# Two layers of a hybrid trunk on one core: attention scores in float32r on 64 rows, GLA in 64-row blocks, token-major columns in groups of 512

## The chip, the cores and the metric

The kernel runs on one core of one Trainium2 chip. The metric is the device time of one execution in microseconds (us); of several executions the median counts. TensorE multiplies matrices, VectorE and ScalarE do the elementwise work, GpSimd very little of it, and SyncE issues the transfers of the weights. In the rows of the trace these are PE (its weight loads PEld), DVE, ACT, POOL and SP.

## What is computed

Two layers over 256 tokens with 1024 channels. Each layer is an FFN, a mixer, a second FFN and a small per-layer embedding, each with a residual and a layer norm. The change lies in the mixer alone:

```python
(a_x, a_y, b_q, b_k, b_v, b_low, b_r,
 c_q, c_k, c_v, c_f, gate_logits) = split(x @ w_in)
y_a = gelu(a_y) * rg_lru(conv(a_x), ...)               # 512 channels
y_b = gla(b_q, b_k, b_v, b_low, w_g2, b_g, norm_g, b_r)
y_c = forgetting_attention(c_q, c_k, c_v, c_f, b_f)
merged = sum(sigmoid(gate_logits)[n] * (y_n @ w_branch[n]) for n in 0, 1, 2)
out = merged @ w_out
# gla: 4 heads, keys of 64, values of 128, chunks of 64 tokens
g = log_sigmoid(b_low @ w_g2 + b_g) / 16; G = cumsum(g within a chunk)
state = scan(exp(G_end), (b_k * exp(G_end - G)).T @ b_v)     # one per chunk
o = (b_q / 8) @ state; y_b = o * rsqrt(mean(o*o) + eps) * norm_g * silu(b_r)
# forgetting attention: 8 heads of 64, queries in two blocks of 128 tokens
F = cumsum(log_sigmoid(c_f + b_f))
s = c_q @ c_k.T / 8 + F[query] - F[key]; y_c = softmax(causal(s)) @ c_v
```

## The kernel before

**Products.** Every large product is made of three products in float32r. A weight piece `raw` arrives by a transfer (16 buffers in turn), ScalarE rounds it to `whi` (line 194), VectorE computes the rest `wlo` (line 195), and TensorE adds hi x hi, hi x lo and lo x hi in PSUM. `mm_tok` (lines 296 to 298) puts tokens on the partitions and weight columns in the free dimension ("token-major"); `mm_feat` (lines 308 to 310) puts 128 weight columns on the partitions and the 256 tokens in the free dimension. The activations are `XH` and `XL`. Products that need more precision with few columns (states, scores, values of attention) are plain float32, which TensorE runs in two passes; a float32 MATMUL of the program therefore counts as x2 in a row of the trace.

**Order.** The instruction order of each engine is the order in which the program is written. The mixer runs a list of units. A unit is one group of weight products (some 48, about 5.7 us each). `run(unit, *new)` adds new chains, lets every live chain do one step, and then emits the unit. A chain is a generator whose `yield` ends a step, so that what a chain needs next from another engine has the time of one unit to be made.

**The mixer's units.** Token-major columns come in `b` groups of 436, 436 and 432 (keys and values of GLA, low-rank decay input, output gate of GLA, forget logits; the array `tm` holds them), and the values of attention in two units `v` of 256. Between these stand two `ax` units (convolution input), two `ay` units (the gate of the first branch), the queries `bq` of GLA, and queries `cq` and keys `ck` of attention, two units each. The chains: `gla_decays` (through `w_g2`, the log-sigmoid at lines 558 to 560 and the exponential at 591 and 593 to the decayed keys), `fox_forget` (the sums F, cast to bfloat16 in three pieces at line 623, transposed at 629), `gla_gate` (line 740), `lru` (lines 671 to 687), `gla_states` (line 718, then the updates over chunks), `gla_out` (line 754, squares, then the products with the norm and the gate at line 260, and the transposes `to_feat` at line 378) and `fox_attend` (scores at lines 786 to 790, softmax, values at 818). After these units come the merge units: 12 gate units and 4 branch units, among whose steps attention is spread.

**GLA products.** The keys are masked to a chunk's half of 128 tokens and the queries `bq` are padded with zeros to 128 rows, so that each product uses 128 rows and 64 columns of the array.

**Scores.** For a head, one bfloat16 product adds -F of the keys, one or two add F of the queries, one adds the causal mask, and one float32 product adds queries times keys; the queries `qz` are padded with zeros to 128 rows, two heads' keys lying above each other. One PSUM bank of 512 columns holds four heads' scores at the first 128 tokens, two at the second: six calls of `fox_attend` per layer, one at every second merge unit.

## Time and profile before

| | |
|---|---|
| median of 3 runs | 1331.17 us (1330.39 to 1331.78) |
| profiled execution, and its span | 1329.03 us, 1327.3 us |
| PE busy | 1306.4 us (98%) |
| PEld busy | 1231.0 us (93%) |
| DVE busy | 825.4 us (62%) |
| ACT busy | 663.9 us (50%) |
| POOL busy | 48.2 us (4%) |
| mean granted clock of TensorE | 0.996 |

The span is what the profile covers of its execution. Busy shares are means over stretches of different kinds. A MATMUL's duration in a row is from its start to its modelled end, and the next begins before that; the price of one among many is the distance of the starts. PEclk is the granted clock as a share of the upper of TensorE's two levels, 2.4 GHz.

### The profile page before, as it was taken

How to read it: one execution, taken by the hardware profiler on the slowest of the kernel's cores; microseconds unless marked ns; L12 is line 12 of the kernel's file. 1: busy time of each engine (PE TensorE's matmuls, PEld its weight loads, DVE VectorE, ACT ScalarE, POOL GpSimd, SP SyncE). 2: the span in 40 equal slices, each digit the busy share in tenths (PEclk: the TensorE clock that was granted, in tenths of full speed). 3: DMA queues.
4: the chain of work that ended last, by engine and by line, in shares of the span. 5: the costliest groups of instructions: out<-in, count | busy, mean ns of one | idle time of the engine just before them, and what ended most of it. 6: DMA issues, size and time to landing. Idle time of an engine off the chain costs nothing. (4 is left out here: it accounts for less than half of the span.)

```text
span 1327.3 us, 22841 instructions
## 1 busy us (share of the span) xinstructions
PE 1306.4 (98%) x9492; PEld 1231.0 (93%) x9492; DVE 825.4 (62%) x1015; ACT 663.9 (50%) x869; POOL 48.2 (4%) x46
## 2 busy tenths in 40 slices
PE   8999999999999999999899999999999999999996
PEld 8999999999999999998799999899999989999985
DVE  6665567675657755557774556676755586555576
ACT  6554436965445444444354445279654444444541
POOL 0000000000001000000000000100000010000000
PEclk9999999999999999999999999999999999999998
DMA  8855736445466466674565667464554555566732
GB/s 273 293 194 190 246 120 236 160 160 162 156 187 199 139 200 184 190 235 168 175 206 182 188 189 244 145 195 154 182 159 147 193 189 168 183 188 188 252 129 72
DMA packets 70216, 246.18 MB, mean 185 GB/s; under 512 B 8160, under 2 KB 8672, under 8 KB 70112
## 3 DMA queue, kind: packets, MB, share of 16 engines
q1 hardware_dynamic: 69824, 244.33, 57.1%
q8 instruction: 74, 1.21, 0.4%
q10 hardware_dynamic: 288, 0.39, 0.1%
q14 instruction: 30, 0.25, 0.1%
HBM read 243.64 MB, written 1.05 MB: 184 GB/s over the span
## 5 line engine op out<-in xcount | busy, mean ns | idle before, releaser
L195 DVE TENSOR_TENSOR wlo<-raw,whi 128x1024 fp32r<-128x1024 f32 (+3 forms) x442 | 541.5, 1234 | 401.1 <-ACT whi L194 399.5
L194 ACT ACTIVATE whi<-raw 128x1024 fp32r<-128x1024 f32 (+3 forms) x442 | 459.6, 1047 | 447.4 <-PE ps L309 263.2
L308 PE MATMUL ps<-XH,whi 128*128 128x256 f32 x1888 | 534.5, 283 | 5.4 <-ACT whi L194 5.4
L310 PE MATMUL ps<-XH,wlo 128*128 128x256 f32 x1888 | 530.5, 281 | 0.4 <-DVE wlo L195 0.4
L309 PE MATMUL ps<-XL,whi 128*128 128x256 f32 x1888 | 530.4, 281 | 0.0
L308 PEld LDWEIGHTS ps<-XH,whi 128*128 128x128 f32 x1888 | 356.6, 189 | 7.8 <-ACT whi L194 5.4
L309 PEld LDWEIGHTS ps<-XL,whi 128*128 128x128 f32 x1888 | 356.4, 189 | 1.4
L310 PEld LDWEIGHTS ps<-XH,wlo 128*128 128x128 f32 x1888 | 356.6, 189 | 0.8 <-DVE wlo L195 0.8
L296 PE MATMUL ps<-whi,XH 128*128 128x256 f32 (+3 forms) x488 | 162.4, 333 | 0.0
L298 PE MATMUL ps<-whi,XL 128*128 128x256 f32 (+3 forms) x488 | 159.0, 326 | 1.3 <-DVE XL L260 1.2
L297 PE MATMUL ps<-wlo,XH 128*128 128x256 f32 (+3 forms) x488 | 159.1, 326 | 0.0
L296 PE MATMUL ps<-whi,hh 128*128 128x512 f32 x368 | 144.6, 393 | 0.0
L298 PE MATMUL ps<-whi,hl 128*128 128x512 f32 x368 | 143.7, 391 | 0.0
L297 PE MATMUL ps<-wlo,hh 128*128 128x512 f32 x368 | 143.3, 389 | 0.0
L298 PEld LDWEIGHTS ps<-whi,XL 128*128 128x128 f32 x488 | 92.0, 189 | 8.2 <-DVE XL L260 1.7
L297 PEld LDWEIGHTS ps<-wlo,XH 128*128 128x128 f32 x488 | 92.4, 189 | 6.2 <-DVE wlo L195 0.3
L296 PEld LDWEIGHTS ps<-whi,XH 128*128 128x128 f32 x488 | 92.0, 188 | 6.6 <-ACT tm L553 0.3
L298 PEld LDWEIGHTS ps<-whi,hl 128*128 128x128 f32 x368 | 69.1, 188 | 15.2 <-DVE hl L260 0.2
L297 PEld LDWEIGHTS ps<-wlo,hh 128*128 128x128 f32 x368 | 69.3, 188 | 13.1
L296 PEld LDWEIGHTS ps<-whi,hh 128*128 128x128 f32 x368 | 69.1, 188 | 12.8
L269 ACT ACTIVATE hh<-w 128x512 fp32r<-128x512 f32 x40 | 25.1, 632 | 71.7 <-DVE w L260 71.7
L308 PE MATMUL ps<-yh,whi 128*128 128x256 f32 x192 | 54.9, 286 | 0.0
(160 smaller groups left out, 953.5 us busy)
## 6 DMA issues: line engine op xcount, KB each, us to landing
raw<-in_wu SPq DMA_DIRECT2D x414, 512.0 KB, 4.1
gb<-in_lnp SPq DMA_DIRECT2D x16, 512.0 KB, 5.9
raw<-in_wu SPq DMA_DIRECT2D x16, 436.0 KB, 4.4
raw<-in_wu SPq DMA_DIRECT2D x8, 432.0 KB, 4.1
xr<-in_xT SPq DMA_DIRECT2D x4, 256.0 KB, 4.4
raw<-in_wu SPq DMA_DIRECT2D x4, 256.0 KB, 4.7
XR<-in_x SPq DMA_DIRECT2D x1, 1024.0 KB, 7.3
wa<-in_lru SPq DMA_DIRECT2D x2, 512.0 KB, 3.8
```

The costliest lines, as they stand in the source:

```text
L194: self.nc.scalar.activation(hi[:, c], raw[:, c], AF.Copy)
L195: (lo or self.nc.vector).tensor_tensor(out=lw[:, c], in0=raw[:, c], in1=hi[:, c].bitcast(F32), op=ALU.subtract)
L269: S.activation(hi, src, AF.Copy)
L296: TE.matmul(o, lhsT=lh[:, k, c], rhs=hi[:, kk, :], start=start and kk == 0, stop=False)
L297: TE.matmul(o, lhsT=lh[:, k, c], rhs=lo[:, kk, :], start=False, stop=False)
L298: TE.matmul(o, lhsT=ll[:, k, c], rhs=hi[:, kk, :], start=False, stop=stop and kk == kt - 1)
L308: TE.matmul(o, lhsT=hi[:, kk, c], rhs=rh[:, k, :], start=start and kk == 0, stop=False)
L309: TE.matmul(o, lhsT=hi[:, kk, c], rhs=rl[:, k, :], start=False, stop=False)
L310: TE.matmul(o, lhsT=lo[:, kk, c], rhs=rh[:, k, :], start=False, stop=stop and kk == kt - 1)
```

## The change

Token-major columns are cut into groups of 512, 512, 280 and 512. The first two are GLA's values (in an array `gv` of their own) and its output gate; the third holds the low-rank input, the forget logits and GLA's keys; the fourth the values of attention. The third moves ahead of the convolution units, the fourth stands where the `v` units stood. Some chains start at another unit.

GLA's products use 64 rows and 64 columns: a chunk's keys and values lie on 64 rows, two chunks in the two row halves and two heads in the two column halves. The keys need one product instead of two masked ones, the queries no padding.

In the scores, one bfloat16 product with per-head factors (`fQ`, made by eight operations of 256 columns on VectorE, and `fK`) adds both forget terms, one adds the mask. Queries and keys of attention are split into two float32r parts, and three products of 64 rows per head replace the float32 one; two heads run in the two row halves of the array, each into a PSUM bank of its own. `fox_attend` handles two banks at a time, so it is called three times per layer, at every fourth merge unit.

```diff
-FOX_EVERY = 2
+FOX_EVERY = 4
...
+
+PB = (0, 512, 1024, 1304, 1816)
+TM_LOW, TM_CF, TM_K, TM_R, TM_CV, TM_N = 0, 16, 24, 280, 792, 1304
+TM_AT = (None, TM_R, TM_LOW, TM_CV)
...
+        b_group(2)
         for i in range(2):
...
         for i in range(2):
             w_in(l, "ay", i, C_AY)
-        for i in range(2):
-            out.append(((l, "v", i), "w_in", (l,), 0, D, C_CV + 256 * i, 256, "k"))
+        b_group(3)
...
-                S.activation(tm[:, t, PB[g]:PB[g + 1]], acc[g, t][:, :n], AF.Copy)
+                S.activation(tm[:, t, TM_AT[g]:TM_AT[g] + n] if g else gv[:, t, :], acc[g, t][:, :n], AF.Copy)
...
-            gla["kd"] = []
-            for h in range(2):
-                k = work()
-                stt(k.rearrange("p (t c) -> p t c", t=2), e.rearrange("p (t c) -> p t c", t=2), chunk[:, h:h + 1],
-                    tm[:, :, TM_K:TM_K + 256], ALU.mult, ALU.mult)
-                gla["kd"].append(k)
+            gla["kd"] = work()
+            tt(gla["kd"].rearrange("p (t c) -> p t c", t=2), e.rearrange("p (t c) -> p t c", t=2), tm[:, :, TM_K:TM_K + 256], ALU.mult)
...
                 V.tensor_copy(part, fc3)
+                V.tensor_copy(fcat[:, :, 32 + 8 * i:40 + 8 * i], fc3)
...
-            fox["f"] = mt([P, T], BF16, "fT")
-            fox["nf"] = mt([P, T], BF16, "nfT")
-            V.tensor_copy(fox["f"], o16[:, :T])
-            ts(fox["nf"], o16[:, :T], -1.0, None, ALU.mult)
+            f = mt([P, T], BF16, "fT")
+            V.tensor_copy(f, o16[:, :T])
+            fox["k"] = mt([P, T], BF16, "fK")
+            ts(fox["k"], f, fox_kmul, fox_kadd, ALU.mult, ALU.add)
+            fox["q"] = mt([P, NH, T], BF16, "fQ")
+            for h in range(NH):
+                if h == NH // 2:
+                    yield
+                ts(fox["q"][:, h, :], f, fox_mul[:, h:h + 1], fox_add[:, h:h + 1], ALU.mult, ALU.add)
...
-        def unit_q(key, dst, h0):
-            o = feat(key)
-            for h in range(4):
-                r = slice((h % 2) * 64, (h % 2) * 64 + 64)
-                S.activation(dst[r, h0 + h, :], o[r, (h // 2) * T:(h // 2 + 1) * T], AF.Copy, scale=0.125)
+        def unit_bq():
+            S.activation(flat(bq), feat((l, "bq", 0)), AF.Copy, scale=0.125)
+
+        def unit_cq(i):
+            o = feat((l, "cq", i))
+            hi, lo = (flat(x[:, 2 * i:2 * i + 2, :]) for x in q2)
+            S.activation(hi, o, AF.Copy, scale=0.125)
+            stt(lo, o, 0.125, hi.bitcast(F32), ALU.mult, ALU.subtract)
...
-            for n in range(4):
-                t, h = n // 2, n % 2
+            for t in range(2):
                 for hd in range(4):
-                    pr, r = hd // 2, slice((hd % 2) * 64, (hd % 2) * 64 + 64)
-                    at = (pr * 2 + t) * P
-                    TE.matmul(od[h][r, at:at + P], lhsT=kd[h][:, t * 256 + hd * 64:t * 256 + hd * 64 + 64],
-                              rhs=tm[:, t, TM_V + hd * P:TM_V + (hd + 1) * P], start=True, stop=True)
+                    for h in range(2):
+                        pr, r, k = hd // 2, rows[hd % 2], rows[h]
+                        at = (pr * 2 + t) * P
+                        TE.matmul(od[h][r, at:at + P], lhsT=kd[k, t * 256 + hd * 64:t * 256 + hd * 64 + 64],
+                                  rhs=gv[k, t, hd * P:(hd + 1) * P], start=True, stop=True)
...
             for t in range(2):
-                o = ps()
-                for hd in range(4):
+                for r in range(2):
...
-                        TE.matmul(o[h * 64:(h + 1) * 64, hd * P:(hd + 1) * P], lhsT=bq[:, hd, n * 64:(n + 1) * 64],
-                                  rhs=gla["st"][n][:, hd // 2, :], start=True, stop=True)
-                os.append(o)
-            for t in range(2):
+                        for e in range(2):
+                            TE.matmul(os[e][rows[h], (2 * t + r) * P:(2 * t + r + 1) * P], lhsT=bq[rows[e], r, n * 64:(n + 1) * 64],
+                                      rhs=gla["st"][n][rows[e], r, :], start=True, stop=True)
...
-            o = ps()
+            os = [ps() for _ in range(2)]
+            at = [slice(j * kn, (j + 1) * kn) for j in range(nh)]
             for j in range(nh):
-                h = g * nh + j
-                c = o[:, j * kn:(j + 1) * kn]
-                TE.matmul(c, lhsT=sel16[:, h, :], rhs=fox["nf"][:, :kn], start=True, stop=False)
-                for i in range(t + 1):
-                    TE.matmul(c[:, i * P:(i + 1) * P], lhsT=fox["f"][:, tk], rhs=sel16[:, h, :], start=False, stop=False)
-                TE.matmul(c[:, tk], lhsT=ident16, rhs=mask16, start=False, stop=False)
-                TE.matmul(c, lhsT=qz[:, h, tk], rhs=kT[:, :t + 1, h // 2, :], start=False, stop=True)
-            mx = small(4, tag="mx")
-            V.tensor_reduce(out=mx[:, :nh], in_=o.rearrange("p (h c) -> p h c", h=nh), axis=mybir.AxisListType.X, op=ALU.max, negate=True)
-            yield
-            pr = work()
-            sums = small(4, tag="sums")
+                for e in range(2):
+                    c = os[e][:, at[j]]
+                    TE.matmul(c, lhsT=fox["q"][:, 2 * (g * nh + j) + e, tk], rhs=fox["k"][:, :kn], start=j == 0, stop=False)
+                    TE.matmul(c[:, tk], lhsT=ident16, rhs=mask16, start=False, stop=False)
...
+                for n, (x, y) in enumerate(((0, 0), (0, 1), (1, 0))):
+                    for e in range(2):
+                        TE.matmul(os[e][:, at[j]], lhsT=q2[x][rows[e], g * nh + j, tk], rhs=fox["kk"][y][rows[e], (g * nh + j) // 2, (g * nh + j) % 2, :kn],
+                                  start=False, stop=n == 2 and j == nh - 1)
...
+        run(lambda: [b_both(2, h) for h in range(2)])
         run(lambda: unit_ax(0))
         run(lambda: unit_ax(1), gla_decays())
-        run(b2)
-        run(lambda: unit_ay(0), lru(0), fox_forget(), gla_gate())
-        run(lambda: unit_ay(1))
-        run(lambda: unit_v(0))
-        run(lambda: unit_v(1), lru(1), gla_states())
-        run(lambda: unit_q((l, "bq", 0), bq, 0))
-        run(lambda: unit_q((l, "cq", 0), qz, 0))
+        run(lambda: unit_ay(0), fox_forget(), gla_gate())
+        run(lambda: unit_ay(1), lru(0))
+        run(lambda: b_both(3, 0))
+        run(lambda: b_both(3, 1), lru(1))
+        run(unit_bq, gla_states())
+        run(lambda: unit_cq(0))
         run(lambda: unit_k(0), gla_out())
...
-        attend = [(0, 0), (0, 1), (1, 0), (1, 1), (1, 2), (1, 3)]
...
-            run(f, *([fox_attend(*attend.pop(0))] if attend and n % FOX_EVERY == 0 else []))
+            run(f, *([fox_attend(*attend.pop(0))] if attend and n % FOX_EVERY == 2 else []))
```

**ScalarE, layer 0, around the exponential of the decays.** The queue before, from two weight splits to the forget logits' second table load. In the names, `whi` and `raw` are weights, `w` work buffers, `s` small ones; ACT_TABLE_LOAD loads the table of the function that follows it.

```order
L194 ACTIVATE whi_2545<-raw_2544 128x1024
L194 ACTIVATE whi_2575<-raw_2574 128x1024
L658 ACT_TABLE_LOAD
L658 ACTIVATE w_2580<-ps_2519 128x512
L591 ACT_TABLE_LOAD
L591 ACTIVATE w_2590<-ps_2582 128x512
L593 ACTIVATE s_2592<-ps_2585 128x8
L558 ACTIVATE w_2597<-s_2513 128x16
L559 ACTIVATE w_2598<-w_2597 128x16
L560 ACT_TABLE_LOAD
L560 ACTIVATE w_2598<-w_2598 128x16
```

The same queue now, from the gelu of the first `ay` unit (line 655) to the second `lru` function's table; the exponential of the decays (line 591 before, 586 now) follows seven rows further.

```order
L655 ACT_TABLE_LOAD
L655 ACTIVATE w_2559<-ps_2498 128x512
L553 ACTIVATE w_2562<-s_2492 128x16
L554 ACT_TABLE_LOAD
L554 ACTIVATE w_2563<-w_2562 128x16
L555 ACT_TABLE_LOAD
L555 ACTIVATE w_2563<-w_2563 128x16
L668 ACT_TABLE_LOAD
L668 ACTIVATE w_2571<-ps_2574,vec 128x256 x2
L668 ACTIVATE w_2572<-ps_2577,vec 128x256 x2
L671 ACTIVATE w_2573<-w_2571,lruc 128x256 x2
L673 ACT_TABLE_LOAD
```

The forget logits' log-sigmoid (lines 553 to 555) and the first `lru` chain (668 to 673) now stand ahead of the decays' exponential; before, the former stood behind it and the latter further ahead.

**VectorE, layer 0, ahead of the GLA output's transposes.** Before, the last twelve rows up to the products with the gate; `wlo` are weight remainders, `yl` the end of an `lru` chain.

```order
L195 TENSOR_TENSOR wlo_3061<-raw_3059,whi_3060 128x1024
L195 TENSOR_TENSOR wlo_3091<-raw_3089,whi_3090 128x1024
L763 TENSOR_REDUCE s_3098<-w_3030 128x4
L763 TENSOR_REDUCE s_3098<-w_3032 128x4
L266 TENSOR_SCALAR s_3098<-s_3098 128x8
L195 TENSOR_TENSOR wlo_3130<-raw_3128,whi_3129 128x1024
L195 TENSOR_TENSOR wlo_3160<-raw_3158,whi_3159 128x1024
L260 TENSOR_TENSOR yl_2256<-w_2402,yh_2255 128x512
L260 TENSOR_TENSOR w_3030<-ps_3012,s_3098 128x512
L260 TENSOR_TENSOR w_3032<-ps_3021,s_3098 128x512
L260 TENSOR_TENSOR w_3030<-w_3030,tm_2072 128x512
L260 TENSOR_TENSOR w_3032<-w_3032,tm_2072 128x512
```

Now, from the first splits behind the state updates on, `fT`, `fK` and `fQ` being the forget factors and `ql` the remainder of attention's queries; the products with the norm and the gate stand some ten rows further.

```order
L198 TENSOR_TENSOR wlo_2841<-raw_2839,whi_2840 128x1024
L198 TENSOR_TENSOR wlo_2871<-raw_2869,whi_2870 128x1024
L623 COPY fT_2879<-ps_150_2876 128x256
L269 TENSOR_SCALAR fK_2881<-fT_2879,cf 128x256
L269 TENSOR_SCALAR fQ_2883<-fT_2879,cf 128x256 x4
L198 TENSOR_TENSOR wlo_2917<-raw_2915,whi_2916 128x1024
L198 TENSOR_TENSOR wlo_2947<-raw_2945,whi_2946 128x1024
L266 SCALAR_TENSOR_TENSOR ql_2073<-ps_2890,qh_2072 128x512
L269 TENSOR_SCALAR fQ_2883<-fT_2879,cf 128x256 x4
L263 TENSOR_TENSOR yl_2253<-w_2396,yh_2252 128x512
L263 TENSOR_TENSOR w_2709<-w_2709,w_2710 128x512
L684 SCALAR_TENSOR_TENSOR w_2475<-w_2708,w_2709 128x256 x2
```

Eight factor products and the queries' remainder stand ahead of the last rows of an `lru` chain, where before only a copy and a negation of the transposed sums stood.

**TensorE, layer 0, scores at the second 128 tokens.** Before, one head's rows; `nfT` and `fT` are the forget sums, `cb` the identity, mask and selection matrices.

```order
L786 LDWEIGHTS cb_85
L786 MATMUL ps_3639<-nfT_2939,cb_85 128x256
L788 LDWEIGHTS fT_2938
L788 MATMUL ps_3639<-cb_85,fT_2938 128x128
L788 LDWEIGHTS fT_2938
L788 MATMUL ps_3639<-cb_85,fT_2938 128x128
L789 LDWEIGHTS cb_85
L789 MATMUL ps_3639<-cb_85 128x128
L790 MATMUL ps_3639<-tm_2072,qz_2074 128x256
```

Now, the end of the bfloat16 rows of the first four heads and their float32r products; `wa` and `gv` hold the two parts of attention's keys, `qh` and `ql` those of its queries.

```order
L796 LDWEIGHTS fQ_2883
L796 MATMUL ps_3606<-fK_2881,fQ_2883 128x256
L797 LDWEIGHTS cb_85
L797 MATMUL ps_3606<-cb_85 128x128
L801 MATMUL ps_3605<-wa_2984,qh_2072 128x256
L801 MATMUL ps_3606<-wa_2984,qh_2072 128x256
L801 MATMUL ps_3605<-gv_2985,qh_2072 128x256
L801 MATMUL ps_3606<-gv_2985,qh_2072 128x256
L801 MATMUL ps_3605<-wa_2984,ql_2073 128x256
L801 MATMUL ps_3606<-wa_2984,ql_2073 128x256
```

The float32r products of two heads alternate, each head's into a bank of its own.

## Rows read from the trace of the kernel before

**Rows 1.** Waits of PE: engine, line, waited for; us in total, times, longest.
```profile
PE ps L378 <- DVE XR L263: 2.1, 1, 2.1
```

**Rows 2.** Windows in layer 0's mixer; columns stand in the first line.
```profile
core 0: us, PE busy (x) PEld busy (x) DVE busy (x) ACT busy (x) POOL busy (x), PEclk, DMA share, GB/s
237.00:267.00 30.00, 30.00 (x257) 29.16 (x256) 18.62 (x30) 29.71 (x46) 2.79 (x2) 1.00 0.50 171
317.00:417.00 100.00, 100.00 (x863) 97.25 (x862) 58.81 (x71) 46.63 (x75) 8.70 (x6) 1.00 0.54 169
```

**Rows 3.** Timeline of PE: start us, us, engine, line, operation, out<-in, count.
```profile
203.31 0.45 PE L296 MATMUL ps<-whi,XH 128*128 128x436 f32 x1
...
214.08 0.28 PE L308 MATMUL ps<-XH,whi 128*128 128x256 f32 x1
...
219.78 0.38 PE L571 MATMUL ps<-cf,tm 128*128 128x128 f32 x2
...
652.63 0.39 PE L298 MATMUL ps<-whi,XL 128*128 128x512 f32 x1
...
654.03 0.40 PE L298 MATMUL ps<-whi,XL 128*128 128x512 f32 x1
```

**Rows 4.** Timeline of DVE and PE at three hand-offs of layer 0's mixer.
```profile
254.55 1.21 DVE L195 TENSOR_TENSOR wlo<-raw,whi 128x1024 fp32r<-128x1024 f32 x1
255.69 1.40 DVE L263 SCALAR_TENSOR_TENSOR w<-w,cf,tm 128x512 f32<-128x512 f32 x2
...
258.32 1.97 PE L718 MATMUL ps<-tm,w 128*64 128x128 f32 x32
...
270.59 0.17 DVE L623 CAST fcat<-s 128x16 bf16<-128x16 f32 x1
...
272.38 0.28 PE L629 MATMUL ps<-cb,fcat 128*128 128x128 bf16 x2
...
295.85 1.28 DVE L260 TENSOR_TENSOR w<-w,tm 128x512 f32<-128x512 f32 x2
...
297.38 0.60 PE L378 MATMUL ps<-cf,w 128*128 128x128 f32 x4
```

**Rows 5.** Timeline of ACT; in brackets the idle time ahead and its releaser.
```profile
226.67 0.58 ACT L647 ACTIVATE axp<-ps 128x512 f32<-128x512 f32 x1
...
232.59 4.59 ACT L194 ACTIVATE whi<-raw 128x1024 fp32r<-128x1024 f32 x4 [0.54 <-PE ps L298]
...
249.65 0.60 ACT L591 ACTIVATE w<-ps 128x512 f32<-128x512 f32 x1
...
252.10 1.99 ACT L194 ACTIVATE whi<-raw 128x1024 fp32r<-128x1024 f32 x2
...
254.12 1.28 ACT L658 ACT_TABLE_LOAD   x1
```

**Rows 6.** Groups by line, DVE, shapes apart: busy us, mean ns | idle us before.
```profile
L266 DVE TENSOR_SCALAR w<-w,s 128x256 f32<-128x256 f32 x16 | 4.9, 351 | 0.3
```

**Rows 7.** Timeline of PE in attention: scores of four heads, values, scores of two.
```profile
303.89 0.22 PE L786 MATMUL ps<-nfT,cb 128*128 128x128 bf16 x1
...
304.06 0.44 PE L790 MATMUL ps<-tm,qz 128*128 128x128 f32 x2
...
305.58 0.36 PE L308 MATMUL ps<-XH,whi 128*128 128x256 f32 x1
...
330.36 0.28 PE L310 MATMUL ps<-XH,wlo 128*128 128x256 f32 x1
330.56 0.66 PE L818 MATMUL ps<-w,tm 128*64 128x128 f32 x8
331.15 0.28 PE L786 MATMUL ps<-nfT,cb 128*128 128x256 bf16 x1
...
332.50 0.47 PE L308 MATMUL ps<-yh,whi 128*128 128x256 f32 x1
```

**Rows 8.** Windows at the border of the two layers, columns as in rows 2.
```profile
654.00:657.30 3.30, 1.20 (x8) 0.73 (x7) 3.27 (x8) 0.00 (x0) 0.92 (x1) 1.00 0.49 159
657.30:660.80 3.50, 3.50 (x12) 2.82 (x11) 2.77 (x4) 1.90 (x3) 0.00 (x0) 0.51 0.35 98
```

More of the change, by code (lines that the diff above doesn't have):

```diff
@@ L145, in constants @@
     chunk = p[:, None] // 64 == np.arange(2)[None, :]
-    cf = np.concatenate([ident, suffix, prefix, ones, chunk], 1).astype(np.float32)
+    head = p[:, None] % 8 == np.arange(8)[None, :]
+    keys, queries = p[:, None] < 24, (p[:, None] >= 32) & (p[:, None] < 56)
+    cf = np.concatenate([ident, suffix, prefix, ones, chunk, head & queries, head & keys, -1.0 * keys, queries], 1).astype(np.float32)
     mask = np.where(p[None, :] <= p[:, None], 0.0, -1e30)
-    sel = ((p[:, None, None] < 24) & (p[:, None, None] % 8 == np.arange(8)[None, :, None])) * np.ones((1, 1, P))
-    cb = np.concatenate([ident, mask, sel.reshape(P, 8 * P)], 1).astype(np.float32)
+    cb = np.concatenate([ident, mask], 1).astype(np.float32)
     return cf, cb
@@ L693, in lru @@
             tt(lo, xc, hi.bitcast(F32), ALU.subtract)
[L696 to L700 removed]
+        def unit_bq():
[5 more added lines that the diff above has]
+            stt(lo, o, 0.125, hi.bitcast(F32), ALU.mult, ALU.subtract)
         def unit_k(i):
[L703 to L705 removed]
+            if i == 0:
+                fox["kk"] = mt([P, 2, 2, T], F32R, "wa"), mt([P, 2, 2, T], F32R, "gv")
+            split(*(x[:, i] for x in fox["kk"]), feat((l, "ck", i)).rearrange("p (j c) -> p j c", j=2))
         yb = yt()
+        rows = [slice(0, 64), slice(64, 128)]
         def gla_states():
@@ new lines, in fox_attend @@
+            for j in range(nh):
+                for n, (x, y) in enumerate(((0, 0), (0, 1), (1, 0))):
+                    for e in range(2):
+                        TE.matmul(os[e][:, at[j]], lhsT=q2[x][rows[e], g * nh + j, tk], rhs=fox["kk"][y][rows[e], (g * nh + j) // 2, (g * nh + j) % 2, :kn],
+                                  start=False, stop=n == 2 and j == nh - 1)
+            mx = [small(4, tag="mx") for _ in range(2)]
+            for e in range(2):
+                V.tensor_reduce(out=mx[e][:, :nh], in_=os[e].rearrange("p (h c) -> p h c", h=nh), axis=mybir.AxisListType.X, op=ALU.max, negate=True)
@@ L799, in fox_attend @@
+            yield
+            pr = [work() for _ in range(2)]
+            sums = [small(4, tag="sums") for _ in range(2)]
+            for e in range(2):
+                for j in range(nh):
+                    S.activation(pr[e][:, at[j]], os[e][:, at[j]], AF.Exp, bias=mx[e][:, j:j + 1], accum_out=sums[e][:, j:j + 1])
             yield
-            V.reciprocal(out=sums[:, :nh], in_=sums[:, :nh])
-            for j in range(nh):
-                c = slice(j * kn, (j + 1) * kn)
-                ts(pr[:, c], pr[:, c], sums[:, j:j + 1], None, ALU.mult)
+            for e in range(2):
+                V.reciprocal(out=sums[e][:, :nh], in_=sums[e][:, :nh])
+                for j in range(nh):
+                    ts(pr[e][:, at[j]], pr[e][:, at[j]], sums[e][:, j:j + 1], None, ALU.mult)
@@ L804, in fox_attend @@
             yield
-            o = ps()
-            for j in range(4):
-                TE.transpose(o[:, j * P:(j + 1) * P], pr[:, j * P:(j + 1) * P], ident)
-            pt = work()
-            S.activation(pt, o, AF.Copy)
-            yield
+            pt = []
+            for e in range(2):
+                o = ps()
+                for j in range(4):
+                    TE.transpose(o[:, j * P:(j + 1) * P], pr[e][:, j * P:(j + 1) * P], ident)
+                pt.append(work())
+                S.activation(pt[e], o, AF.Copy)
+                yield
@@ L814, in fox_attend @@
             for j in range(nh):
-                h = g * nh + j
+                p = g * nh + j
                 for i in range(t + 1):
                     b = j * (t + 1) + i
-                    TE.matmul(oy[(h % 2) * 64:(h % 2) * 64 + 64, (h // 2) * P:(h // 2 + 1) * P],
-                              lhsT=tm[:, i, TM_CV + h * 64:TM_CV + (h + 1) * 64], rhs=pt[:, b * P:(b + 1) * P], start=i == 0, stop=i == t)
-            if (g + 1) * nh == NH:
+                    for e in range(2):
+                        h = 2 * p + e
+                        TE.matmul(oy[rows[e], p * P:(p + 1) * P], lhsT=tm[:, i, TM_CV + h * 64:TM_CV + (h + 1) * 64],
+                                  rhs=pt[e][:, b * P:(b + 1) * P], start=i == 0, stop=i == t)
+            if (g + 1) * nh == NH // 2:
                 if t == 0:
@@ L1003, in late_loads @@
         V.memset(mhalf, -0.5)
-        for i in range(2):
-            w = zp.tile([P, D], F32, tag="z", name=nm("cst"))
-            load(w[:, :640], a["cb"][:, i * 640:(i + 1) * 640])
-            V.tensor_copy(flat(cb16[:, 5 * i:5 * i + 5, :]), w[:, :640])
+        w = zp.tile([P, D], F32, tag="z", name=nm("cst"))
+        load(w[:, :256], a["cb"])
+        V.tensor_copy(flat(cb16), w[:, :256])
         lru_constants()
```

73 lines of the change are left out of this document (33 added, 40 removed).

## The prediction

> **What bounds the kernel now.** I read the waits of TensorE first. Its longest wait inside the program is 2.1 us [rows 1], at the border of the two layers; inside the mixers, where the whole change lies, the view lists none. The stretches of layer 0's mixer agree: TensorE is busy for all of each of them [rows 2]. So the mixer's time is that of TensorE's products, and work taken from it is time won, as long as nobody else is late. Who is nearly late stands in the same rows: between 237 and 267 us ScalarE is busy 29.71 of 30.00 us [rows 2]. There it splits weights, runs the gates' functions and reloads its function tables, and it is kept out of TensorE's way only by slack. That slack I read from three hand-offs [rows 4]. The decayed keys are ready when the pair that begins at 255.69 ends, at 257.09, and the state products begin at 258.32: slack 1.2 us. The last cast of the forget sums ends at 270.76, their transposes begin at 272.38: 1.6 us. The GLA output's last product with its gate ends at 297.13, its transposes begin at 297.38: 0.25 us. The question is which way these three numbers go.
>
> **TensorE's work, per layer.** Prices first. A product of 436 columns takes 0.199 us (54 between 203.31 and 214.08), one of 256 takes 0.119 (48 between 214.08 and 219.78), one of 512 takes 0.233 (6 between 652.63 and 654.03) [rows 3]. The group of 280 columns is not shown; between the neighbours it is 0.130, bounds 0.119 and 0.199; I take 0.130. Token-major columns: groups 0 and 1 grow by 96 x 0.034 = 3.3 us; group 2 falls from 48 x 0.200 to 48 x 0.130, -3.4; the 96 products of 256 columns (11.4) become 48 of 512 (11.2). Together -0.3: the columns are the same.
>
> GLA states took 1.97 us [rows 4], and the GLA output has the same 32 passes. Four quarters instead of two halves give 1.0 at best and 1.97 at worst; I take 1.4, so -1.1 for both.
>
> Attention: the scores of four heads at the first 128 tokens take 1.69 us (303.89 to 305.58), of two heads at the second 128 they take 1.35 (331.15 to 332.50) [rows 7]; two and four of these make 8.8 us. Now they are 24 bfloat16 products of 128 columns and 8 of 256, at 0.056 us for 128 columns (three from 303.89 to 304.06 [rows 7]), 2.3 us, and 48 fp32r products on half the rows, in 24 pairs. If a pair costs what one product of 256 columns costs, that is 24 x 0.119 = 2.9. Three times the array changes its shape for them and back. A change there and back costs 0.23 at the eight products from 330.56, the value products: from 330.36 to 331.15 less 0.12 for the product ahead and 0.44 for four pairs of passes at 0.11; with a loss at the next large product I take 0.34, 1.0 in all. Sum 6.2, so -2.6. If a pair's members follow each other, 2.9 more, a gain of nothing; if the twelve short pairs cost half, 0.7 less. The value products come in three groups of eight instead of six of four, which saves three changes of shape, -0.7. So the merge stretch gains 3.3, bounds 0.4 and 4.0.
>
> Alone on TensorE the change would thus be worth -0.3 - 1.1 - 3.3 = -4.7 us per layer.
>
> **What it moves.** The new order puts group 2 (keys, low-rank decay, forget logits) ahead of the two conv units, and the values of attention, once two units of 256, last. The decay chain starts behind group 2, and the state products still follow one unit after its end. On TensorE the state products come at 258.32 + 3.3 - 3.4 + (11.2 - 5.7: all of the value columns are now ahead of them, once half) + 0.6 (the forget sums' products moved ahead) = 264.3.
>
> Their operand: the second conv unit ends 3.3 + 6.2 = 9.5 us later than before, so ScalarE's copy of it moves from 226.67 to 236.2 [rows 5]. From there to the exponential of the decays it was 22.98 us (to 249.65). In the new queue ten table loads stand in this piece, before six: the gate's tanh, the small log-sigmoid of the forget logits and a second gelu now alternate with other functions ahead of that exponential. A load is 1.28 us and 0.13 around it [rows 5]: +5.7. A gelu and three small ones, +1.0. Against that two copies and an idle moment go, -1.5, and of six weight splits four are left: four took 4.59 from 232.59 with a pause in it and two take 1.99, as those from 252.10; four without a pause are 4.0, so -2.6. Sum +2.6: the exponential starts at 261.8. Then come itself and two splits on ScalarE (0.60 and 1.99 [rows 5], of which a row's last 0.1 overlaps the next: 2.5), the second's counterpart on VectorE (1.14, from 254.55 to 255.69 [rows 4]) and one keys' product instead of two (0.70 to its end): ready at 266.1. **First wait: 1.8 us.**
>
> Forget sums: TensorE continues at 266.1 with 1.4 of states and 5.7 of the query unit and arrives at 273.2. ScalarE has, from the exponential's start on, 2.5 as above + three table loads 4.2 + six gate functions and a square root 3.5 + a split, a copy, a split 2.4 = 12.6, that is 274.4; then VectorE's split 1.14, and nine small operations where six took 1.2, 1.7: ready at 277.3. **Second wait: 4.1 us.**
>
> GLA output: behind the last cast VectorE now has, without a pause, eight weight splits (9.1), sixteen operations of 512 columns (0.65 each by the 1.28 of the pair at 295.85 [rows 4], 10.4), four scans (2.6), ten of 256 columns for the new per-head forget factors and their source and two for the gate (a row of this size shows 0.351 [rows 6], half of 0.65 is 0.32, and the bfloat16 ones move half the bytes, for which half of that again is the lower bound; I take 0.26, 3.2), eight state updates of 128 columns (between a quarter of 0.65 and 0.351: 0.25, 2.0) and one small (0.2): 27.5 us, so 304.8. Three things made it longer: both gate chains' ends and the state updates stand behind the cast instead of ahead of it, the query and key remainders are VectorE's now, and the eight factors are new. TensorE arrives after the transposes (0.1), a unit (5.7), the GLA output (1.5) and three units (17.1), at 301.7. **Third wait: 3.1 us.**
>
> At no cost I take the fills of the padded queries that go (GpSimd's, far from any wait), the weights' transfers (as many pieces and bytes per layer as before) and the second PSUM bank that a score group now holds for a unit: the trace lists no wait of TensorE for a bank, and were one needed, it would wait for the exponentials, some 1 us on ScalarE.
>
> So the transposes that began at 297.38 begin at 304.8, +7.4; behind them the merge stretch has ScalarE at 46.63 and VectorE at 58.81 of 100 us [rows 2], which covers the moved work there, and TensorE's -3.3 counts in full. Net +4.1 per layer, +8.2 for two. The profiled execution took 1329.03 us for a span of 1327.3; it lies 2.1 under the median of 1331.17. Against the median: 1339.
>
> The Trainium skill (TensorEngine Tiling (Array Packing), Performance Considerations, PSUM Bottleneck) says that packing makes TensorE faster and leaves the emptying of PSUM as slow as it was. This trace has the same with 29.71 of 30.00 us; by the rule the GLA's gain ahead of the third hand-off is worth nothing, as in the sum above, where without it the sum would be the first rival's.
>
> **Rivals.** (1) The waits don't come, because ScalarE's queue isn't as full as summed: then TensorE alone counts, -4.7 x 2, 1322. For it: the six weight splits that the queue holds can be done earlier when TensorE frees their buffers earlier, and the trace hides such slack. Against it: 29.71 of 30.00. It decides when the chain from 236.2 to 304.8 is 4.1 of its 69 us shorter; no change is measured there, and faster lies beyond. (2) The halves of the array don't work side by side: +2.8 per layer in the scores, 1345. No row here has products on half the rows; for the halves of the columns the eight passes from 330.56 fill little more than half of what eight of 0.11 would. (3) The clock: after 2.1 us in which TensorE waited, it was granted 0.51 for 3.5 us, its lower level of 1.2 GHz [rows 8]. A product of 256 columns would cost about 0.21 there, so such a stretch costs 1.5 us. Behind the first two waits that shortens the next wait and costs nothing; behind the third it costs 1.5 per layer, 1342. The skill (TensorE: Matmul & The Clock Gate, Part 1) has the lower level as the default to which an idle array returns; that fits rows 8 and would make this rival likelier.
>
> **How the numbers follow.** The sum as it stands 0.55, rival 1 0.17, rival 2 0.14, rival 3 0.14. Own range of the likeliest: 1.5 us either way for the two queues and the merge's bounds, per layer, which is 1333 to 1346. The range that should hold 8 in 10 is 1332 to 1347. A measurement of this kernel tells about 0.2%, 2.7 us. Rival 1 splits into faster 0.10 and no difference 0.07; of the sum's low end 0.03 more is no difference. Slower 0.80.
>
> **What would show it.** Right: waits of TensorE on VectorE at the state products, at the transposes of the forget sums and at those of the GLA output, some 2, 4 and 3 us, in both layers; ScalarE without pause from about 236 to 276, VectorE from there to about 305; the stretch behind shorter by about 3. Wrong: no such waits, or the time lost behind the GLA transposes, in the score products.

## The result, and the profile after

The changed kernel takes 1345.06 us (1344.75 to 1346.97), the kernel before 1330.78 us beside it: a ratio of 1.0113 (1.01 to 1.0125), 14 to 15 us slower. 1339 was forecast, 1332 to 1347 the range. Its profiled execution spans 1343.4 us.

The three waits are there. The view of TensorE's waits (line waited for: us in total, times, longest us) of the changed kernel lists them twice each, once per layer, at the forget sums' transposes, the GLA states and the GLA output's transposes; in [rows 1] they were absent.

```profile
PE ps L621 <- DVE fcat L615: 4.3, 2, 2.2
PE ps L719 <- DVE w L263: 3.3, 2, 1.6
PE ps L382 <- DVE XR L266: 2.7, 1, 2.7
PE ps L780 <- DVE w L263: 1.9, 2, 1.0
```

In the timeline of layer 0 they stand at the hand-offs of [rows 4], with the rows of VectorE that end them (in brackets the idle time ahead, and its releaser).

```profile
266.08 2.36 DVE L198 TENSOR_TENSOR wlo<-raw,whi 128x1024 fp32r<-128x1024 f32 x2 [1.21 <-ACT whi L197]
268.36 0.68 DVE L263 TENSOR_TENSOR w<-w,tm 128x512 f32<-128x512 f32 x1
...
269.19 1.10 PE L719 MATMUL ps<-gv,w 64*64 64x128 f32 x32 [1.65 <-DVE w L263]
...
275.81 1.23 DVE L198 TENSOR_TENSOR wlo<-raw,whi 128x1024 fp32r<-128x1024 f32 x1 [6.77 <-ACT whi L197]
279.66 0.17 DVE L615 CAST fcat<-s 128x16 bf16<-128x16 f32 x1
279.89 0.28 PE L621 MATMUL ps<-cb,fcat 128*128 128x128 bf16 x2 [2.15 <-DVE fcat L615]
...
306.37 0.74 DVE L263 TENSOR_TENSOR w<-w,tm 128x256 f32<-128x256 f32 x2
306.93 0.68 PE L780 MATMUL ps<-cf,w 128*128 128x128 f32 x4 [0.95 <-DVE w L263]
```

VectorE waits for ScalarE ahead of the first hand-off (1.21 us) and again ahead of the second (6.77 us), so ScalarE's queue is behind the first two. From 277.24 us to the third hand-off the timeline shows no idle time of VectorE, so its own queue is behind the third. Windows over the products that follow the three waits (columns as in [rows 2]) show the clock.

```profile
270.20:277.70 7.50, 7.50 (x52) 7.30 (x48) 1.69 (x2) 7.46 (x15) 0.00 (x0) 0.77 0.20 78
279.90:287.20 7.30, 7.30 (x50) 7.30 (x50) 7.16 (x16) 3.66 (x5) 0.00 (x0) 0.77 0.22 81
306.90:313.00 6.10, 6.07 (x51) 6.03 (x52) 5.13 (x9) 2.30 (x5) 0.00 (x0) 1.00 0.50 179
```

Behind the first and the second wait the mean granted clock is 0.77, that is, TensorE runs at its lower level of 1.2 GHz for part of the stretch; behind the third it is 1.00.

But 4.75 us of waits per layer, less what the products save, are not 14 us for two layers. The rest is in a place where nothing was changed. The timeline of TensorE shows 96 products with XH or XL in the first FFN of layer 0, at a granted clock of 1.00: first and last of them in the changed kernel.

```profile
65.93 0.28 PE L312 MATMUL ps<-XH,whi 128*128 128x256 f32 x1
...
77.34 0.28 PE L314 MATMUL ps<-XH,wlo 128*128 128x256 f32 x1
```

Their starts are 11.41 us apart, 95 steps, 0.1201 us per product. The same 96 took 0.1187 each before, also at 1.00:

```profile
64.30 0.28 PE L308 MATMUL ps<-XH,whi 128*128 128x256 f32 x1
...
75.58 0.28 PE L310 MATMUL ps<-XH,wlo 128*128 128x256 f32 x1
```

There are 5664 such products in the program (three groups of 1888), so 0.0014 us each make 7.9 us. Hence the first four experiments ask what sets this price.

### The profile page after: what moved, and what is told of

The parts are those of the page before. It is cut to its first block, busy times and chain, and to the rows that moved or that the text cites. A ratio compares the mean times of both kernels' runs of the same rounds, so it can differ in the third digit from the quotient of the medians.

```text
span 1343.4 us, 22627 instructions
## 1 busy us (share of the span) xinstructions
PE 1311.0 (98%) x9380; PEld 1225.9 (91%) x9380; DVE 830.1 (62%) x1050; ACT 662.5 (49%) x851; POOL 46.5 (3%) x42
## 5 line engine op out<-in xcount | busy, mean ns | idle before, releaser
L198 DVE TENSOR_TENSOR wlo<-raw,whi 128x1024 fp32r<-128x1024 f32 (+2 forms) x442 | 539.1, 1228 | 409.3 <-ACT whi L197 407.8
L197 ACT ACTIVATE whi<-raw 128x1024 fp32r<-128x1024 f32 (+2 forms) x442 | 459.3, 1046 | 445.6 <-PE ps L313 269.6
L312 PE MATMUL ps<-XH,whi 128*128 128x256 f32 x1888 | 540.8, 286 | 6.0 <-ACT whi L197 6.0
L313 PE MATMUL ps<-XL,whi 128*128 128x256 f32 x1888 | 536.2, 284 | 0.0
L300 PE MATMUL ps<-whi,XH 128*128 128x512 f32 (+2 forms) x456 | 156.8, 344 | 0.0
L302 PE MATMUL ps<-whi,XL 128*128 128x512 f32 (+2 forms) x456 | 153.9, 338 | 1.3 <-DVE XL L263 1.3
L301 PE MATMUL ps<-wlo,XH 128*128 128x512 f32 (+2 forms) x456 | 153.9, 337 | 0.8 <-DVE wlo L198 0.8
L302 PEld LDWEIGHTS ps<-whi,XL 128*128 128x128 f32 x456 | 86.2, 189 | 11.6 <-DVE XL L263 1.7
L301 PEld LDWEIGHTS ps<-wlo,XH 128*128 128x128 f32 x456 | 86.2, 189 | 10.7 <-DVE wlo L198 1.5
L300 PEld LDWEIGHTS ps<-whi,XH 128*128 128x128 f32 x456 | 86.2, 189 | 9.7 <-ACT whi L197 0.5
```

The source lines that it names most:

```text
L197: self.nc.scalar.activation(hi[:, c], raw[:, c], AF.Copy)
L198: (lo or self.nc.vector).tensor_tensor(out=lw[:, c], in0=raw[:, c], in1=hi[:, c].bitcast(F32), op=ALU.subtract)
L300: TE.matmul(o, lhsT=lh[:, k, c], rhs=hi[:, kk, :], start=start and kk == 0, stop=False)
L301: TE.matmul(o, lhsT=lh[:, k, c], rhs=lo[:, kk, :], start=False, stop=False)
L302: TE.matmul(o, lhsT=ll[:, k, c], rhs=hi[:, kk, :], start=False, stop=stop and kk == kt - 1)
L312: TE.matmul(o, lhsT=hi[:, kk, c], rhs=rh[:, k, :], start=start and kk == 0, stop=False)
```

## Experiments

Ratios are to the kernel before, run beside each kernel on the same chip, with 95% intervals. "Distance" is the start of the weight buffers less that of XH, modulo 256 bytes, as the program's allocation has them; all buffers of `whi` and `wlo` lie whole multiples of 256 bytes apart, and so do XH and XL. "Price" is that of one product with XH or XL and 256 columns, from the first and the last start of 96 in a row in an FFN. In the FFNs of one kernel such stretches differ by up to 0.0002; in other stretches of a kernel a second price occurs, on which more stands under "Two more distances".

| kernel | distance | price, us | time, us | ratio |
|---|---|---|---|---|
| before | 96 | 0.1187 | 1330.78 | 1 |
| changed | 160 | 0.1201 | 1345.06 | 1.0113 (1.01 to 1.0125) |
| a_pad64 | 224 | 0.1167 | 1328.77 | 0.9991 (0.9981 to 1.0) |
| b_pad64 | 160 | 0.1201 | 1337.79 | 1.0056 (1.0041 to 1.0071) |
| a_pad32 | 192 | 0.1178 | 1331.08 | 1.0008 (0.9998 to 1.0017) |
| a_pad96 | 0 | 0.1199 | 1342.52 | 1.0089 (1.0074 to 1.0105) |
| b_pad128 | 224 | 0.1167 | 1320.32 | 0.9929 (0.9915 to 0.9944) |
| a_front64 | 160 | 0.1201 | 1344.78 | 1.0103 (1.0088 to 1.0119) |
| b_prod | 224 | 0.1167 | 1307.13 | 0.9835 (0.9821 to 0.985) |
| b_prod_192 | 64 | 0.1178 | 1304.99 | 0.981 (0.9791 to 0.983) |
| b_prod_0 | 128 | 0.1200 | 1323.45 | 0.9945 (0.993 to 0.9959) |
| a_order | 224 | 0.1167 | 1311.49 | 0.9865 (0.9851 to 0.988) |
| a_order_seq | 224 | 0.1167 | 1314.65 | 0.9894 (0.9878 to 0.9911) |
| a_gate | 224 | 0.1167 | 1331.67 | 1.0009 (0.9999 to 1.0018) |

**Where the weights lie.** The change made the constants 1984 bytes shorter per partition (the selection matrices went), and every buffer behind them moved. An unused array puts them elsewhere; 16, 8 and 24 elements in the changed kernel (a_pad64, a_pad32, a_pad96), 16 and 32 in the kernel before (b_pad64, b_pad128).

```diff
     mhalf = const.tile([P, 8], F32, name="mhalf")
+    pad = const.tile([P, 16], F32, name="pad")
```

> The changed kernel with 64 unused bytes per partition behind its constants, so that every weight buffer starts 64 bytes later, at the same offset within 128 bytes as in the kernel before. Theory placement: the products that stream XH or XL cost 0.1201 us in the changed kernel and 0.1187 before, at the same granted clock, because the weights lie at another offset; 5664 of them make 8 us. Expected: 0.1187 again, 1337 us. Rival, the new order of instructions or transfers slows them: 0.1201 still, 1345 us.

> The kernel before with the same 64 unused bytes, which puts its weight buffers at the changed kernel's offset. Theory placement: 0.1201 us per product with XH or XL, 1339 us. Rival, order or transfers: 0.1187 and 1331 us.

> The changed kernel with 32 unused bytes: weight buffers at offset 64 within 128 bytes, which neither kernel had. Theory placement: a price per product other than 0.1201, on either side of it, and a time 4 us or more off 1345. Rival, order or transfers: 0.1201 and 1345 us.

> The changed kernel with 96 unused bytes: weight buffers at offset 0 within 128 bytes, as XH and XL have. Theory placement: a price per product other than 0.1201, a time 4 us or more off 1345. Rival, order or transfers: 0.1201 and 1345 us.

Three of the four went with the place as expected. The fourth, a_pad96, was to be 4 us or more off 1345; it is 2.5 off, and its price of 0.1199 is so near 0.1201 that it tells little by itself. The kernel before became 7.8 us slower by 64 unused bytes and nothing else. The changed kernel became some 16 us faster by as many; the price it got, 0.1167, was lower than that of either kernel, so the figure of 1337 was wrong and the mechanism right. By the price alone it would be 19 us (5664 times 0.0034); some of that went into the three waits, which are 11.6 us there where they were 9.5. The same pair of rows as above, in a_pad64, and then in b_pad64:

```profile
64.24 0.28 PE L313 MATMUL ps<-XH,whi 128*128 128x256 f32 x1
...
75.32 0.28 PE L315 MATMUL ps<-XH,wlo 128*128 128x256 f32 x1
```

```profile
65.75 0.28 PE L309 MATMUL ps<-XH,whi 128*128 128x256 f32 x1
...
77.16 0.28 PE L311 MATMUL ps<-XH,wlo 128*128 128x256 f32 x1
```

11.08 us and 11.41 us for the 95 steps; the second is the changed kernel's value.

> The kernel before with 128 unused bytes per partition behind its constants. Its weight buffers then start at 96 modulo 256, as in the padded changed kernel that ran at 0.1167 us per product; unpadded they start at 224. Theory that the place modulo 256 bytes sets the price: 0.1167 instead of 0.1187, 5664 products, 1330 - 11 = 1319 us. Rival, the place modulo 128 decides and the 0.1167 is something of the changed kernel: 0.1187 and 1330 us.

1320.32 us at 0.1167. So 128 bytes matter, and the place modulo 128 doesn't say enough.

**Place or distance.** In a_front64 the unused bytes stand ahead of XH, so that weights and XH move together.

```diff
+    pad = const.tile([P, 16], F32, name="pad")
     XH = const.tile([P, KD, T], F32R, name="XH")
```

> The changed kernel with the 64 unused bytes ahead of XH and XL instead of behind the constants, so that weights, XH and XL all move by 64 bytes. Weights then lie at 96 modulo 256 as in the version that ran at 0.1167 us per product, but at the same distance from XH as in the unpadded changed kernel (160 modulo 256). Theory that the distance between the two operands decides: 0.1201 and 1345 us. Rival, the weights' own place decides: 0.1167 and 1329 us.

1344.78 us, 0.1201: the price goes with the distance between the operands, not with the weights' own place.

This makes b_pad64 the fair partner of the changed kernel: the same distance, the same price, the old code. Against it the change costs 1.0113 / 1.0056 = 1.0057, 7.6 us; at the distance of 224, a_pad64 against b_pad128, 0.9991 / 0.9929 = 1.0062, 8.2 us. The two agree, as each ratio is known to some 0.0015, 2 us.

**The products alone.** b_prod has the new GLA blocks, the new scores and the three attention calls, in the old column groups and the old order of units and chains. Against the changed kernel:

```diff
-PB = (0, 512, 1024, 1304, 1816)
...
+PB = (0, 436, 872, 1304)
...
-        run(lambda: [b_both(2, h) for h in range(2)])
         run(lambda: unit_ax(0))
         run(lambda: unit_ax(1), gla_decays())
-        run(lambda: unit_ay(0), fox_forget(), gla_gate())
-        run(lambda: unit_ay(1), lru(0))
-        run(lambda: b_both(3, 0))
-        run(lambda: b_both(3, 1), lru(1))
-        run(unit_bq, gla_states())
+        run(b2)
+        run(lambda: unit_ay(0), lru(0), fox_forget(), gla_gate())
+        run(lambda: unit_ay(1))
+        run(lambda: unit_v(0))
+        run(lambda: unit_v(1), lru(1), gla_states())
+        run(unit_bq)
...
+    pad = const.tile([P, 16], F32, name="pad")
```

> The products of the change alone (64-row GLA blocks, 64-row scores, three attention calls), in the column groups and the order of units of the kernel before, weight buffers at 96 modulo 256. Two weight copies per token block are cut in two, since GLA's values have an array of their own. Theory that the moved units cause the three waits: none of them above 0.5 us, and the products' gain of some 6 us per layer in full: 12 under the kernel before with 128 unused bytes, 1307 us. Rival, the new work on VectorE (factors, remainders) is enough for a late GLA output: a wait of 1 to 3 us at its transposes per layer, and 1311 us or more.

1307.13 us, 13.2 under b_pad128, and none of the three waits is in the list of TensorE's waits; what it lists are the program's start and the borders of blocks, with 2.7 us as the longest behind the start.

```profile
PE ps L312 <- ACT whi L196: 6.9, 1, 6.9
PE ps L382 <- DVE XR L265: 2.7, 1, 2.7
PE ps L302 <- DVE XL L262: 1.3, 1, 1.3
PE ps L301 <- DVE wlo L197: 0.8, 1, 0.8
```

So the products are a gain, VectorE's new work included, and the moved groups and chains turn it into a loss: a_pad64, with these products in the new groups and the new order at the same distance, takes some 21 us more.

**The chains' order.** a_order keeps the new column groups and, beside the 64 unused bytes, moves chains alone.

```diff
             yield
+            yield
+            yield
             o16 = psp.tile([P, 1024], BF16, tag="ps", name=nm("ps16"))
...
                     tt(x, x, gate, ALU.mult)
             yield
+            yield
...
-        run(lambda: unit_ay(0), fox_forget(), gla_gate())
-        run(lambda: unit_ay(1), lru(0))
+        run(lambda: unit_ay(0))
+        run(lambda: unit_ay(1), fox_forget(), lru(0))
...
-        run(unit_bq, gla_states())
+        run(unit_bq, gla_states(), gla_gate())
...
-        run(lambda: unit_k(0), gla_out())
-        run(lambda: unit_cq(1))
+        run(lambda: unit_k(0))
+        run(lambda: unit_cq(1), gla_out())
...
-            run(f, *([fox_attend(*attend.pop(0))] if attend and n % FOX_EVERY == 2 else []))
+            run(f, *([fox_attend(*attend.pop(0))] if attend and n % FOX_EVERY == 3 else []))
```

> The changed kernel with 64 unused bytes and another order of its chains: the decays' chain has ScalarE to itself (forget logits start one unit later, the GLA gate four units later), forget sums get two more units, GLA's output starts one unit later and its transposes one unit more, attention starts one merge unit later. No work differs. Theory that the chains' order makes the waits: none of the three above 0.5 us, and with them go the stretches at the lower clock; 1306 to 1311 us against 1328.8 for the same kernel in its own order. Rival, ScalarE and VectorE simply have too much to do there: the waits come back in other places, 1322 us or more.

1311.49 us, some 17 under a_pad64 and half a us above the upper end of what was expected. Two of the three waits are gone, the third is 1.1 us in one layer and 0.3 in the other, where 0.5 at most was expected:

```profile
PE ps L784 <- DVE w L263: 1.4, 2, 1.1
```

So the order of the chains makes some 17 of the 21 us. What makes the other 4, by which a_order lies above b_prod, wasn't tried.

**One step of it.** a_gate moves the gate's chain alone, beside the 64 unused bytes, to test the sum over ScalarE's queue.

```diff
-        run(lambda: unit_ay(0), fox_forget(), gla_gate())
+        run(lambda: unit_ay(0), fox_forget())
...
-        run(unit_bq, gla_states())
+        run(unit_bq, gla_states(), gla_gate())
```

> The changed kernel with 64 unused bytes behind the constants, and the GLA gate's chain started four units later (at the queries of GLA), nothing else moved. Theory that table loads and small functions queued ahead of the decays' exponential cause the first wait: one load and two functions, 2.4 us, leave that queue; the wait at the state products falls from 2.0 us to 0.3 or less per layer, and 1328.8 us becomes 1323 to 1326. Rival, the weight splits set that time: the wait stays above 1.5 us, and the time within 2 us of 1328.8.

The wait at the state products went, as expected, and the time did not: 1331.67 us, by the ratios (1.0009 and 0.9991) 2.4 more than a_pad64. The waits moved on. First TensorE's waits in a_pad64, then in a_gate:

```profile
PE ps L781 <- DVE w L263: 4.4, 2, 3.0
PE ps L720 <- DVE w L263: 4.0, 2, 2.0
PE ps L622 <- DVE fcat L616: 3.2, 2, 2.2
```

```profile
PE ps L622 <- DVE fcat L616: 6.9, 2, 3.5
PE ps L781 <- DVE w L263: 6.3, 2, 3.2
```

The sum over the queue was right: from the copy of the second conv unit to the decays' exponential ScalarE takes 22.94 us in a_gate, 25.40 in the changed kernel and in a_pad64, 2.46 less where 2.4 were counted. The rows are the copy and the exponential, in the changed kernel and then in a_gate:

```profile
239.04 0.58 ACT L644 ACTIVATE axp<-ps 128x512 f32<-128x512 f32 x1
...
264.44 0.60 ACT L586 ACTIVATE w<-ps 128x512 f32<-128x512 f32 x1
```

```profile
235.07 0.59 ACT L645 ACTIVATE axp<-ps 128x512 f32<-128x512 f32 x1
...
258.01 0.60 ACT L587 ACTIVATE w<-ps 128x512 f32<-128x512 f32 x1
```

The Trainium skill (ScalarE: Activation LUTs, What ACT_TABLE_LOAD costs) has 1.28 us for the load and 1.38 more for a drain; by that, as an estimate, 3.8 us would have left the queue. The trace has the 1.28 and no drain: in a_gate the load that stands at 243.95 ends at 245.23, and its function begins at 245.25.

What was wrong was to stop there. The gate's own operations on VectorE and GpSimd now fall between the forget sums and the GLA output, where VectorE is the one that is late. Its rows there in a_gate, with GpSimd's:

```profile
283.97 1.29 DVE L266 SCALAR_TENSOR_TENSOR tm<-w,tm 128x512 f32<-128x512 f32 x2
...
284.89 5.05 POOL L747 TENSOR_TENSOR tm<-tm,ng 128x512 f32<-128x512 f32 x2 [53.95 <-DVE tm L266]
...
288.05 2.48 DVE L269 TENSOR_SCALAR fQ<-fT,cf 128x256 bf16<-128x256 bf16 x4
```

Two products more, 1.3 us, and four factor products that take 2.48 us beside GpSimd's products, where the same four take 1.11 us with GpSimd idle (GpSimd's two took 5.05 us, 2.73 in the changed kernel):

```profile
293.13 1.11 DVE L269 TENSOR_SCALAR fQ<-fT,cf 128x256 bf16<-128x256 bf16 x4
```

That row is of the changed kernel. The Trainium skill (GPSIMD Engine Reference, Specifications) has the two engines share their interfaces to SBUF, with contention for instructions of VectorE that run in a 2-port mode or read two inputs from SBUF. The two rows agree if the factor products are of the first kind, which no row shows. Of the second kind are the weight splits, and there the trace doesn't agree: two of them took 2.36 us beside the same GpSimd products (at 285.18) and 2.35 without (at 280.09).

**Two halves of the array.** a_order_seq is a_order with the score products of a pair's first heads all ahead of those of the second.

```diff
-            for j in range(nh):
-                for n, (x, y) in enumerate(((0, 0), (0, 1), (1, 0))):
-                    for e in range(2):
+            for e in range(2):
+                for j in range(nh):
+                    for n, (x, y) in enumerate(((0, 0), (0, 1), (1, 0))):
```

> The same as the reordered kernel, but the float32r score products of the first head of every pair all come ahead of those of the second, so that consecutive products use the same rows. Theory that two halves work side by side: 24 pairs per layer now cost 1.5 to 2.7 us more, the time is 3 to 5 us above the reordered kernel's. Rival, a pair is cheap for another reason: the same score stretches and the same time within 1 us.

1314.65 us, 3.2 more. One group of twelve products at the second 128 tokens takes 0.90 us in pairs and 1.25 us in sequence; the timeline shows the first rows and the product behind, in a_order and then in a_order_seq.

```profile
333.30 0.39 PE L805 MATMUL ps<-wa,qh 64*128 64x256 f32 x2
333.53 0.28 PE L805 MATMUL ps<-gv,qh 64*128 64x256 f32 x2
...
334.20 0.38 PE L313 MATMUL ps<-XH,whi 128*128 128x256 f32 x1
```

```profile
333.80 0.38 PE L805 MATMUL ps<-wa,qh 64*128 64x256 f32 x1
334.02 0.28 PE L805 MATMUL ps<-gv,qh 64*128 64x256 f32 x1
...
335.05 0.38 PE L313 MATMUL ps<-XH,whi 128*128 128x256 f32 x1
```

**Two more distances**, in b_prod with 40 and 56 elements of unused array instead of 16.

> The products of the change alone, in the order before, with weights at 192 modulo 256, 64 behind XH's place. At 224 behind XH's place the same kernel took 1307.1 us with 0.1167 us per product; 0, 96, 160 and 192 gave 0.1199, 0.1187, 0.1201 and 0.1178. The places form no line, so no price is forecast beyond their bounds: 0.1167 to 0.1201, 1307 to 1327 us.

> The same with weights at 0 modulo 256, 128 from XH's place. The bounds as for the other: 0.1167 to 0.1201, 1307 to 1327 us. If only the distance modulo 128 mattered, it would be as with distance 0: 0.1199 and 1326 us.

At a distance of 128 the price in the FFNs is that of 0, at 64 that of 192; but 96 and 224, 0.1187 and 0.1167, differ. So it isn't the distance modulo 128 alone. Nor is it the distance alone. b_prod_192 has the lowest median of all (its interval overlaps b_prod's), though its price in the FFNs is 0.0011 above b_prod's. In its trace the same kind of product has a second price, at the same distance and the same granted clock of 1.00: in the first stretch of the program and in many of the mixers' stretches it is 0.113 to 0.114. First and last of 96 in a row near the start:

```profile
19.15 0.28 PE L312 MATMUL ps<-XH,whi 128*128 128x256 f32 x1
...
29.91 0.28 PE L314 MATMUL ps<-XH,wlo 128*128 128x256 f32 x1
```

10.76 us for 95 steps are 0.1133 each. Over all steps from one such product to the next at full clock, steps over 0.15 us left out, the mean step is 0.1167 in b_prod_192 and 0.1168 in b_prod, so the two agree; in b_prod_0 it is 0.1194, which makes 15 of its 16 us above b_prod. The kernel before has two prices as well, 0.1187 and, in many stretches of its mixers, 0.1173. What in the chip reads two operands more slowly at one distance than at another, and what switches between two prices at one distance, wasn't tried.

## Why the prediction was right, and where not

The time lies in the range, and the direction was right. The difference is two things of one size: 7.8 us by the weights' place (b_pad64), which the prediction doesn't have, and 7.6 or 8.2 by the change itself (at distances of 160 and 224), for which it had 8.2. The range held only because it was wide enough for a term that wasn't in it.

**The step that failed** is the one on unit prices: a product of 256 columns was taken at 0.119 from [rows 3], for both kernels. For the 5664 products that stream XH or XL it became 0.1201, because the shorter constants moved the weights. That is 8 us in products that the diff doesn't touch, and the list of what was taken at no cost has no line for it.

**The three hand-offs** can be held against b_pad64, at one price. Its rows at the same places, none with a wait:

```profile
260.98 1.20 PE L719 MATMUL ps<-tm,w 128*64 128x128 f32 x18
...
275.04 0.29 PE L630 MATMUL ps<-cb,fcat 128*128 128x128 bf16 x2
...
300.34 0.60 PE L379 MATMUL ps<-cf,w 128*128 128x128 f32 x4
...
409.64 0.28 PE L309 MATMUL ps<-yh,whi 128*128 128x256 f32 x1
```

The last row begins the last branch products of layer 0; in the changed kernel it is this:

```profile
412.06 0.28 PE L312 MATMUL ps<-yh,whi 128*128 128x256 f32 x1
```

The first wait was forecast at 1.8 us and is 1.65. The exponential was to come 25.6 us behind the conv copy (22.98 + 2.6), and comes 25.40 behind it. From the first hand-off to the last cast 11.2 us were summed, and it is 10.6 (269.19 to 279.83); from the cast to the GLA output's transposes 27.5, and it is 27.1 (279.83 to 306.93). These links are the prediction's best part. TensorE's way between them was mis-sized: the second wait is 2.15 for 4.1, the third 0.95 for 3.1, because the clock fell behind the first two waits, 1.5 us in each unit (7.35 for 5.85 in b_pad64, and 7.42 for 5.92). That had been said to shorten the next wait and to cost nothing by itself, and so it was, but the waits' sizes hadn't been lowered for it. The GLA transposes come 6.6 us later than in b_pad64, for 7.4.

**The products** saved more than was summed. GLA's states take 1.03 us to the next product (269.19 to 270.22) and its output as much, where each took 1.90 in b_pad64: 1.7 us per layer for 1.1. b_prod has 6.6 us per layer for GLA and scores together, where 4.4 was summed.

**The merge stretch** saved 4.2 us (6.6 at its start, 2.4 at its end), for 3.3 with bounds of 0.4 and 4.0: mis-sized, a little beyond its upper bound. The scores of eight heads at the first 128 tokens take 2.47 us, where two groups of four took 1.69 each [rows 7]; a pair takes 0.11, where 0.12 was taken:

```profile
313.64 0.22 PE L796 MATMUL ps<-fK,fQ 128*128 128x128 bf16 x1
...
314.79 0.27 PE L801 MATMUL ps<-gv,qh 64*128 64x128 f32 x2
314.90 0.28 PE L801 MATMUL ps<-wa,ql 64*128 64x128 f32 x2
...
316.11 0.39 PE L312 MATMUL ps<-XH,whi 128*128 128x256 f32 x1
```

So layer 0 loses 2.2 us in the mixer (2.4 less 0.2 by which it began later), and layer 1 as much (215.23 us for 213.03 between the same two places), 4.4 in all where 8.2 was summed. The remaining 3.1 of the 7.5 us between the two profiled spans (1343.4 and 1335.9) lie outside the mixers, in code that is the same. Some 1.9 of them arise at the border of the layers, where TensorE waits 0.8 us for a weight remainder, a wait that b_pad64 lacks, and 2.7 us for the layer norm, 2.1 in b_pad64; b_prod, in the old order, has both waits too. Why wasn't settled. That the whole came out at 8 is thus partly chance.

**Rivals.** The first, that the waits don't come, fell: they came, in both layers. The second, that the halves don't work side by side, fell by the pairs at 0.11 and by a_order_seq. The third, the lower clock behind the third wait, didn't come in the changed kernel (1.00 in that window of layer 0); behind the first two it came as foretold. It is no dead rival, though: in a_pad64, the same program with 64 unused bytes, the third wait of layer 0 was 2.96 us, and the mean granted clock behind it 0.54, that is, nearly the lower level throughout. The wait, and the window behind it with columns as in [rows 2]:

```profile
302.46 1.08 PE L781 MATMUL ps<-cf,w 128*128 128x128 f32 x4 [2.96 <-DVE w L263]
```

```profile
302.90:309.00 6.10, 6.10 (x33) 6.10 (x32) 4.05 (x7) 1.23 (x3) 0.00 (x0) 0.54 0.58 196
```

**The full queue.** The prediction set ScalarE's 29.71 of 30.00 us beside the emptying of PSUM. By the rows of that stretch 11.5 us of them are nine table loads and 8.1 are weight splits; what reads PSUM is 6.2 us. The queue was full, but not by the emptying of PSUM.

## What to carry to other kernels

Before the cost of a change is summed, look at what it does to the allocation: an array that shrinks moves all that lie behind it, and a product in another block of the program can change its price by 1 to 3%, thousands of times over. When two kernels are compared, compare the price of products that the change does not touch first, and pad until it agrees. Where one engine's wait is removed, follow the chain to its last hand-off: it was in series here, and only moving several chains at once, or leaving their order alone, kept the gain of the products.

## What was not expected of the hardware

- In the FFNs the price of one product with 256 columns of float32r runs from 0.1167 to 0.1201 us at a granted clock of 1.00, with the distance of its two operands in SBUF modulo 256 bytes: 0.1199 at 0, 0.1178 at 64, 0.1187 at 96, 0.1200 at 128, 0.1201 at 160, 0.1178 at 192, 0.1167 at 224.
- At one distance such products can have two prices: in b_prod_192 (distance 64) 0.1178 in the FFNs and 0.1133 in the first stretch of the program, both at 1.00.
- Products with the other moving operand, yh, kept 0.1183 or 0.1184 in the last branch of a layer in all these kernels; it moved along with the weights, so its distance to them never changed.
- Two products of 256 columns on the two row halves take 0.12 us together, as long as one of them that follows another on the same rows.
- Four operations of VectorE on 256 columns of bfloat16 took 2.48 us beside a product of GpSimd and 1.11 us without one; two weight splits took 2.36 us beside it, as without.
